# Queries and keys of the first attention group by seven block products, banks in turns, and the pooling projection from its last group to its first

## Chip, cores and metric

The kernel runs on one core of one Trainium2 chip. The metric is device time in microseconds of one execution: 1033.13 us, the median of three runs (1032.23 to 1033.27). TensorE (PE) multiplies, VectorE (DVE), ScalarE (ACT) and GpSimd (POOL) do the elementwise work, SyncE (SP) issues nearly all transfers.

## The reference, cut to what matters

One layer of a hybrid trunk on x of shape (1, 512, 1024), float32. A normed input u is projected by w_in into queries, keys and values of three attention groups (six heads of 64 each), a pooling input, the parts of a state space branch, and gates:

```
u = rmsnorm(x, ln1_g[i])
proj = u @ w_in[i]
q, k, v, pool_in, z, xbc, dt_raw, gate_pre = jnp.split(proj, split_idx, axis=-1)
...
scores = jnp.einsum("bhnqd,bhnkd->bhnqk", qb, kb).astype(jnp.float32) * scale + bias[:, None]
...
for gi, w in enumerate(POOL_WINDOWS):
    ...
    outs.append((c - shifted) / cnt - uf[..., sl])
d = jnp.stack(outs, axis=2).astype(u.dtype)
y = jnp.einsum("bsgc,gcd->bsgd", d, w_grp).reshape(b, s, POOL_WIDTH)
```

The attention scale is 0.125. The four pooling windows are 2, 4, 8 and 16 tokens, each on 256 of the 1024 pooling channels. After the three branches come a gated merge, an output projection, a gated convolutional FFN and a last norm.

## The kernel before, in words

Every float32 product is made of three TensorE products: each operand is split into a rounded high part and a low part (`wh`, `wl` of a weight, `uh`, `ul` of u), and `mm3` (L229) issues high by high, high by low, low by high, in this order, so that `wl` is read only in the last third of each chunk.

The work is a list of jobs (class `Job`, L73), written by `program()` (L1423) and run by the loop at L1634. A job has a weight tile `raw`, a `body` that issues its matmuls and evacuations, perhaps a `form` (the tile to use in place of a loaded one) and a `then` (what follows its split). Ahead of the body of job n, `prepare` (L1641) issues `low` of job n+1 (VectorE: raw minus high, L216, and then the job's `then`), `cast` of job n+2 (ScalarE: the high part, L196, in two halves that wait for the next two steps), and `fetch` of job n+3 (the load, L175; two `raw` buffers). TensorE, ScalarE, VectorE and GpSimd execute in the order in which the program issues; SyncE's order is left to the framework. `step()` (L157) is called between chunks of matmuls: it lets every generator in `running` and one of `waiting` go on by one `yield`. So elementwise work is spread over chunks.

The order of jobs: 4 of the pooling projection (`jobs_a`, L256, two chunks of 128 channels each, 24 matmuls of 512 columns a chunk), 2 of the values of group 0 (`v_jobs`, L588, 400 columns, four blocks of 12 matmuls each), 3 of queries and keys of group 0 (`qk_jobs`, L631), one that multiplies the pooled channels by pool_w (`pool_out_job`, L877), attention of group 0 between the chunks of the w_b projection, gates, the values of groups 1 and 2 (`v_pair`, L608), queries and keys of group 1 (`qk_sevens`, L650), and so on. The first two pooling jobs are issued by `begin` (L1543), interleaved with the turning of x.

`pool_evac(m)` (L852) takes pooling chunk m: ScalarE copies it out of the bank (L856), GpSimd doubles a window sum as often as its window needs (an addition L860 and a copy L861 for each doubling, then L863): once for m 0 and 1, twice for 2 and 3, three times for 4 and 5, four times for 6 and 7. Two steps later VectorE subtracts (`pd`, L869), ScalarE casts (L871), VectorE takes the low part (`pdl`, L872).

`v_pair` and `qk_sevens` halve u by tokens and by channels and use seven products of half-size blocks in place of eight. Their left sides are sums of blocks of u: `sums_of_u(p)` (L403) for p 0 to 3 makes them on VectorE (two additions L408, four half-width ones L326 to L329, two subtractions L335 and L336) with two ScalarE casts, in four steps, and before the change it runs once, beside the w_b jobs. The weights' sums are made in place by `diff` (L340, 128x1536). Two of the four weight quarters come into `W` (pool `ypool`, two buffers), two into `raw`. The products leave the bank by ScalarE copies and are added up on VectorE.

`attend(g)` (L720) adds the bias to the scores: for groups 0 and 2 the queries have been scaled by 0.125 on their way out of the bank (L642), for group 1 the scores are scaled as the bias is added (L758).

Of the kernel before, what the change touches and what calls it, by code (L numbers as in the profile page):

```python
# [13 lines left out]
OP = mybir.AluOpType  # L14
# [69 lines left out]
def trunk(ctx: ExitStack, tc, out, x, rel_bias, ln1_g, w_in, b_gate, w_a, pool_w, pool_scale, w_b,  # L84
# [258 lines left out]

    def sevens(quarter, c, side, W, emit):

        r1, r2, r3, r5 = {}, {}, {}, {}

        def job(j, load, form, use):  # L350
            def body(ws):
                wh, wl = ws
                parts = side(j)
                for i in range(2):
                    ps = MM("pb")
                    o = slice(i * P, (i + 1) * P)
                    mm3(ps[:, :c], lambda k: wh[:, k, :], lambda k: wl[:, k, :],
                        lambda k: parts[k][0][:, o], lambda k: parts[k][1][:, o], range(4), flip=True)
                    use(i, ps[:, :c])
                step()  # L360
            new = Job([load] if load is not None else [], 4, c, body)
            new.form = form
            if load is None:
                new.load = lambda: None
            return new

        def keep(r, name):
            def use(i, ps):
                r[i] = T(name)[:, :c]
                act.copy(r[i], ps)  # L370
            return use

        def p5(i, ps):
            keep(r5, "r5")(i, ps)
            dve.tensor_tensor(r2[i], r2[i], ps, OP.add)

        def p6(i, ps):
            dve.tensor_tensor(r1[i], r1[i], ps, OP.add)
            emit(0, 1, i, r1[i], r2[i])

        def p7(i, ps):
            r3[i] = T("r3")[:, :c]
            dve.tensor_tensor(r3[i], r1[i], ps, OP.add)
            emit(1, 1, i, r3[i], r5[i])

        one = job("A11", quarter(0, 0), None, keep(r1, "r1"))
        two = job("A12", quarter(1, 0), None, lambda i, ps: emit(0, 0, i, r1[i], ps))
        three = job(4, None, lambda: W[1], keep(r2, "r2"))
        one.then = lambda: diff(one.raw, W[0], one.raw)
        three.then = lambda: diff(W[0], W[1], W[0])  # L390
        two.then = lambda: diff(W[1], W[1], one.raw)
        yield one
        yield three
        yield two
        yield job(1, None, lambda: one.raw, p5)
        yield job(2, None, lambda: W[1], p6)
        yield job(3, None, lambda: W[0], p7)
        yield job("A22", None, lambda: diff(two.raw, two.raw, W[1]),
                  lambda i, ps: emit(1, 0, i, r3[i], ps))

# [18 lines left out]
    QUARTER = {"A11": (0, LO), "A12": (1, LO), "A22": (1, HI)}  # L419

# [187 lines left out]
    def v_pair():  # L608

        c, W = C_V + 384, []  # L610
        rows_ = lambda c0: w_in[:, c0:c0 + 384].rearrange("(k two p) c -> two p k c", two=2, p=P)
        quarter = lambda two, h: rows_(c + 384 * h)[two]

        def load():
            for two in range(2):
                W.append(ypool.tile([P, 4, S], F32, name="w3", tag="xs")[:, :, :384])
                sp.dma_start(W[two], quarter(two, 1))

        def emit(hi, right, i, a, ps):
            g, tb = 1 + right, 2 * hi + i  # L620
            t = T(f"v{g}")
            dve.tensor_tensor(t[:, :384], a, ps, OP.add)

            for n in range(4):
                if (g, n) not in V:
                    V[g, n] = T(f"vr{g}")
                sp.dma_start(V[g, n][32 * tb:32 * tb + 32, :384], t[n:P:4, :384])

        return load, sevens(quarter, 384, side_u, W, emit)
# [20 lines left out]
    def qk_sevens(g):  # L650


        W = []
# [3 lines left out]
        r1, r2, r3, r5 = {}, {}, {}, {}  # L657

        def load():
            for two in range(2):  # L660
                W.append(ypool.tile([P, 4, S], F32, name="w3", tag="xs")[:, :, :384])
                sp.dma_start(W[two], quarter(two, 1))

        def job(j, raw, form, use):
            def body(ws):
                wh, wl = ws
                parts = side_u(j)
                for i, ms in enumerate(chunks):
                    ps = MM("pq")
                    for n, m in enumerate(ms):  # L670
                        o = slice(m * P, (m + 1) * P)
                        mm3(ps[:, 256 * n:256 * n + 256], lambda k: wh[:, k, o], lambda k: wl[:, k, o],
                            lambda k: parts[k][0], lambda k: parts[k][1], range(4))
                    use(i, ps[:, :256 * len(ms)])
                step()
            new = Job([raw] if raw is not None else [], 4, 384, body)
            new.form = form
            if raw is None:
                new.load = lambda: None
            return new  # L680

        def keep(r):
            def use(i, ps):
                r[i] = T("rq")[:, :ps.shape[-1]]
                act.copy(r[i], ps)
            return use

        def emit(which, hi, i, a, b):

            for n, m in enumerate(chunks[i]):  # L690
                if (which, g, m) not in QK:
                    QK[which, g, m] = T(f"{which}{g}")
                view = (grouped if which == "q" else plain)(QK[which, g, m], g)
                piece = lambda t: perm(t[:, 256 * n:256 * n + 256], g)
                dve.tensor_tensor(view[:, :, 64 * hi:64 * hi + 64], piece(a), piece(b), OP.add)

        def p5(i, ps):
            keep(r5)(i, ps)
            dve.tensor_tensor(r2[i], r2[i], ps, OP.add)

        def p6(i, ps):
            dve.tensor_tensor(r1[i], r1[i], ps, OP.add)
            emit("k", 0, i, r1[i], r2[i])

        def p7(i, ps):
            r3[i] = T("rq")[:, :ps.shape[-1]]
            dve.tensor_tensor(r3[i], r1[i], ps, OP.add)
            emit("k", 1, i, r3[i], r5[i])

        one = job("A11", quarter(0, 0), None, keep(r1))  # L710
        two = job("A12", quarter(1, 0), None, lambda i, ps: emit("q", 0, i, r1[i], ps))
        three = job(4, None, lambda: W[1], keep(r2))
        one.then = lambda: diff(one.raw, W[0], one.raw)
        three.then = lambda: diff(W[0], W[1], W[0])
        two.then = lambda: diff(W[1], W[1], one.raw)
        return load, [one, three, two, job(1, None, lambda: one.raw, p5), job(2, None, lambda: W[1], p6),
                      job(3, None, lambda: W[0], p7), job("A22", None, lambda: diff(two.raw, two.raw, W[1]),
                                                          lambda i, ps: emit("q", 1, i, r3[i], ps))]

    def attend(g):  # L720
# [7 lines left out]
        def item(h, nb, bank):  # L728
# [21 lines left out]
            if g == 0 and total == 384:  # L750
                dve.tensor_tensor(sb[:, :256], ps[:, :256], b, OP.add)
                dve.tensor_tensor(sb[:, 256:384], ps[:, 256:384], b[:, P:], OP.add)
# [3 lines left out]
            else:  # L756
                n = len(bank)
                dve.scalar_tensor_tensor(sb.rearrange("p (n c) -> p n c", n=n),  # L758
                                         ps.rearrange("p (n c) -> p n c", n=n), 0.125 if g == 1 else 1.0,
# [663 lines left out]
    def program():  # L1423
        yield from jobs_a(w_in, C_POOL, 8, uhk, ulk, KD, pool_evac)
        yield Call(lambda: waiting.append(rows_of_bias()))
        yield from v_jobs(0)
        yield from qk_jobs(0)
        yield from pool_out_job()
        yield Call(lambda: attend(0))
        yield Call(lambda: waiting.insert(3, ssd_prep()))  # L1430
        for i, job in enumerate(branch_jobs(1, w_b, YB, 8, more=range(7))):
# [3 lines left out]
        load, pair = v_pair()  # L1435
        yield Call(load)
        yield from gate_jobs(1, 0, SPLIT)
        loads, qk = qk_sevens(1)
        for i, job in enumerate(pair):
            yield job  # L1440
            if i == 4:
                yield Call(loads)
# [100 lines left out]
    def begin(n, lo, hi, between=lambda early: None):  # L1543
# [157 lines left out]
```

## Time and profile before

| what | value |
|---|---|
| median of three runs | 1033.13 us (1032.23 to 1033.27) |
| the profiled execution | 1032.69 us, span in the profile 1030.9 us |
| busy in the span: TensorE, VectorE, ScalarE, GpSimd | 1019.8, 702.7, 490.2, 132.8 us |
| granted TensorE clock, mean | 0.999 |
| moved by DMA | 117.62 MB |
| largest VectorE group: low parts of weights, L216 | 95 instructions, 220.3 us |

The span is shorter than the execution by what lies before the first and after the last recorded instruction. In the views, a row of the chain or of the timeline begins with its start and its length in us, counted from the start of the span; merged rows end with the count of instructions. A square bracket tells idle time of the engine ahead of the row and who ended it. A row of windows gives for each engine its busy time in the stretch and its instructions. GpSimd's and VectorE's busy time includes time in which an instruction has been issued and waits inside the engine.

### The profile page before, as it was taken

The page shows a single profiled execution, that of the slowest core. Times are in us where ns is not written, and L with a number is a line of the kernel's source. Part 1 is how long each engine was busy: PE and PEld are TensorE (multiplying, and loading weights), DVE is VectorE, ACT ScalarE, POOL GpSimd, SP SyncE. Part 2 cuts the span into 40 slices and gives each one's busy share as a digit, 9 for nine tenths or more (in the row PEclk, how much of TensorE's full clock was granted, in tenths as well). Part 3 has the DMA queues.
Part 4 walks back from the last instruction along what each step waited for, and adds up shares of the span by engine and source line. Part 5 has one row for each costly group of instructions (what it writes and reads, how often), then busy time and mean ns, then how long its engine had stood idle before and what let it go on. Part 6 is the DMA issues. An engine that isn't in the chain of part 4 may idle for free.

```text
span 1030.9 us, 13254 instructions
## 1 busy us (share of the span) xinstructions
PE 1019.8 (99%) x5276; PEld 858.0 (83%) x5276; DVE 702.7 (68%) x932; ACT 490.2 (48%) x784; POOL 132.8 (13%) x114
## 2 busy tenths in 40 slices
PE   8999999999999999999999999999999999999997
PEld 8998877899888887788888888898888888888885
DVE  6553566788756648666688856767778668685756
ACT  6432545454674363567575324545444434433434
POOL 1770000000000001100044501101111100111002
PEclk9999999999999999999999999999999999999999
DMA  8444312034322354551253625543232233421322
GB/s 270 135 129 137 108 57 75 31 88 138 123 82 82 93 158 108 133 144 44 80 151 128 203 82 203 171 142 121 82 122 83 84 117 112 138 82 41 123 82 82
DMA packets 113357, 117.62 MB, mean 114 GB/s; under 512 B 5236, under 2 KB 97207, under 8 KB 113296
## 3 DMA queue, kind: packets, MB, share of 16 engines
q1 hardware_dynamic: 112703, 115.92, 36.4%
q8 instruction: 41, 0.67, 0.3%
q10 hardware_dynamic: 592, 0.86, 0.2%
q14 instruction: 21, 0.16, 0.1%
HBM read 112.97 MB, written 2.22 MB: 112 GB/s over the span
## 4 chain that ended last, share of the span: by engine, by line
PE 91%; DVE 4%; ACT 3%; issue 1%; DMA 1%; ACTq 0%; DVEq 0%
PE pa L237 30%; PE pu L237 22%; PE pb L237 12%; PE pd L237 7%; PE pqk L237 6%; PE pa L1552 2%; PE pq L237 2%; PE pu L1356 1%; PE ps L743 1%; PE pt L772 1%; PE ppw L237 1%; PE po L784 1%; DVE xs L1133 1%; DVE wl L216 1%; PE py L1057 1%
## 5 line engine op out<-in xcount | busy, mean ns | idle before, releaser
L216 DVE TENSOR_TENSOR wl<-raw,wh 128x2048 fp32r<-128x2048 f32 (+3 forms) x95 | 220.3, 2320 | 53.3 <-ACT wh L196 43.5
L196 ACT CAST wh<-raw 128x1024 fp32r<-128x1024 f32 (+3 forms) x188 | 187.6, 1017 | 48.3 <-DVE raw L341 18.0
L1251 DVE SCALAR_TENSOR_TENSOR hc<-pu,fcol,hc 128x510 f32<-128x510 f32 x88 | 65.8, 748 | 56.0 <-ACT hc L1248 54.4
L237 PE MATMUL pa<-uh,wh 128*128 128x512 f32 x384 | 98.4, 398 | 0.0
L237 PE MATMUL pa<-ul,wh 128*128 128x512 f32 x384 | 94.9, 389 | 0.0
L237 PE MATMUL pa<-uh,wl 128*128 128x512 f32 x384 | 94.8, 389 | 0.0
L237 PEld LDWEIGHTS pa<-ul,wh 128*128 128x128 f32 x384 | 72.1, 188 | 15.1
L237 PEld LDWEIGHTS pa<-uh,wl 128*128 128x128 f32 x384 | 72.1, 188 | 15.0
L237 PE MATMUL pu<-uh,wh 128*128 128x512 f32 (+1 forms) x352 | 83.6, 379 | 0.0
L237 PE MATMUL pu<-uh,wl 128*128 128x512 f32 (+1 forms) x352 | 83.5, 379 | 0.0
L237 PE MATMUL pu<-ul,wh 128*128 128x512 f32 (+1 forms) x352 | 83.5, 379 | 0.0
L237 PEld LDWEIGHTS pa<-uh,wh 128*128 128x128 f32 x384 | 70.3, 188 | 14.8 <-issue 1.0
L237 PEld LDWEIGHTS pu<-ul,wh 128*128 128x128 f32 x352 | 64.2, 188 | 12.5
L237 PEld LDWEIGHTS pu<-uh,wl 128*128 128x128 f32 x352 | 64.2, 188 | 12.5
L237 PEld LDWEIGHTS pu<-uh,wh 128*128 128x128 f32 x352 | 64.1, 188 | 12.4
L1248 ACT ACTIVATE hc<-pu,fcol,fcol 128x512 f32<-128x512 f32 x40 | 31.2, 780 | 80.5 <-PE pu L237 80.5
L1256 POOL TENSOR_TENSOR hc<-hc 128x512 f32<-128x512 f32 x22 | 30.8, 1402 | 289.1 <-DVE hc L1251 252.0
L1025 POOL TENSOR_TENSOR xd<-xc,dtz 128x512 f32<-128x512 f32 x6 | 6.4, 1063 | 355.9 <-issue 307.5
L765 ACT ACTIVATE sb<-sb,nmls 128x128 f32<-128x128 f32 (+1 forms) x72 | 30.1, 419 | 30.4 <-DVE nmls L762 17.7
L1149 ACT ACTIVATE sg<-pa,col 128x512 f32<-128x512 f32 x24 | 16.5, 688 | 45.5 <-PE pa L237 45.4
L1253 ACT ACTIVATE hc<-hc 128x512 f32<-128x512 f32 x22 | 13.9, 632 | 39.9 <-DVE hc L1251 39.9
L907 DVE SCALAR_TENSOR_TENSOR xs<-pa,col,xs 128x509 f32<-128x509 f32 (+2 forms) x24 | 18.0, 749 | 18.7 <-ACT xs L903 18.2
(373 smaller groups left out, 1868.0 us busy)
## 6 DMA issues: line engine op xcount, KB each, us to landing
raw<-in_w_in_dram SPq DMA_DIRECT2D x25, 1024.0 KB, 5.5
raw<-in_ffn_w_up_dram SPq DMA_DIRECT2D x22, 1024.0 KB, 5.2
raw<-in_w_o_dram SPq DMA_DIRECT2D x8, 1024.0 KB, 6.6
raw<-in_ffn_w_down_dram SPq DMA_DIRECT2D x8, 1024.0 KB
raw<-in_w_in_dram SPq DMA_DIRECT2D x14, 512.0 KB, 3.9
raw<-in_w_in_dram SPq DMA_DIRECT2D x6, 768.0 KB
raw<-in_w_b_dram SPq DMA_DIRECT2D x4, 1024.0 KB, 5.2
al<-ad SPq DMA_DIRECT2D x16, 256.0 KB, 7.7
```

What stands on the lines that cost most here:

```text
L196: act.copy(job.high[:, :, o], job.raw[:, :, o])
L216: (eng or dve).tensor_tensor(l[:, :, o], job.raw[:, :, o], h[:, :, o].bitcast(F32), OP.subtract)
L237: pe.matmul(ps, l, r, start=first and n == 0, stop=last and n == total - 1, skip_group_check=onto)
L743: pe.matmul(pss[i][:, o:o + w * P], q[r, n * P:(n + 1) * P], k[r, kb * P:(kb + w) * P], start=True, stop=True)
L765: act.activation(sb[:, off:off + w * P], sb[:, off:off + w * P], AF.Exp, bias=nm[:, n, h:h + 1], accum_out=ls[:, n, h:h + 1])
L907: dve.scalar_tensor_tensor(t[:, sh:], ps[:, :S - sh], col[:, o_cw + 12 * k + m:o_cw + 12 * k + m + 1], t[:, sh:], OP.mult, OP.add)
L1149: act.activation(s, ps, AF.Sigmoid, bias=col[:, o:o + 1])
L1248: act.activation(t, ps, AF.Identity, bias=ff["c1"][:, ff["b"] + m:ff["b"] + m + 1], scale=fw(2, m))
L1251: dve.scalar_tensor_tensor(t[:, sh:], ps[:, :S - sh], fw(k, m), t[:, sh:], OP.mult, OP.add)
L1253: act.activation(t, t, AF.Silu)
L1256: pool.tensor_tensor(a, a, t, OP.mult)
L1552: pe.matmul(first[2 * n + j][:, lo:hi], a[:, k, j * P:(j + 1) * P], b[:, k, lo:hi], start=a is wh and b is uh and k == 0, stop=a is wl and ...
```

## The change

- Queries and keys of group 0 are no longer made by three jobs of 512-column chunks but by `qk_sevens(0)`: seven products of 36 matmuls of 256 columns. For this `sums_of_u` is run a second time, early: it is started ahead of the third pooling job. The two quarters in `W` are loaded at that place, and their difference is taken (`first`) ahead of the second job of the values of group 0.
- `v_pair` and `qk_sevens` are both written over `in_banks`. Two pairs of banks, A and B, are used in turns by the seven products, in the order one, three, six, five, seventh, two, four; the products six, seventh and four add onto what bank pair A holds. A result goes straight to its place by a ScalarE copy and later pieces are added there by VectorE, in place of separate copies of each product.
- The queries of group 0 leave unscaled; `attend(0)` scales the scores as it adds the bias.
- The four pooling jobs run in reverse, so that chunks come as 6, 7, 4, 5, 2, 3, 0, 1.

The core of the diff (the two functions that it replaces are printed above):

```diff
+    def in_banks(quarter, c, outs, both, chunks=None):
...
+        W, A, B = [], [], []
...
+        def job(j, raw, form, banks, use, onto=False, between=None):
+            def body(ws):
+                wh, wl = ws
+                parts = side_u(j)
+                if not A:
+                    for b in (B, A):
+                        b.extend(MM("pq") for _ in range(2))
+                for i in range(2):
+                    for n, m in enumerate(chunks[i] if chunks else (i,)):
+                        o = slice(m * P, (m + 1) * P)
+                        if chunks:
+                            mm3(banks[i][:, 256 * n:256 * n + 256], lambda k: wh[:, k, o],
+                                lambda k: wl[:, k, o], lambda k: parts[k][0], lambda k: parts[k][1],
+                                range(4), onto=onto or n > 0)
+                        else:
+                            mm3(banks[i][:, :c], lambda k: wh[:, k, :], lambda k: wl[:, k, :],
+                                lambda k: parts[k][0][:, o], lambda k: parts[k][1][:, o],
+                                range(4), onto=onto, flip=True)
+                    outs(*use, i, banks[i][:, :256 * (n + 1) if chunks else c])
+                    if j == 1:
+                        both(i)
+                    if i == 0 and between:
+                        between()
+                    step()
...
+        one = job("A11", quarter(0, 0), None, A, (0, 0, False),
+                  between=lambda: diff(W[1], W[1], one.raw))
+        three = job(4, None, lambda: W[1], B, (1, 0, False))
+        six = job(2, None, lambda: one.raw, A, (1, 0, True), onto=True)
+        five = job(1, None, lambda: W[1], B, (1, 1, False))
+        seventh = job(3, None, lambda: W[0], A, (1, 1, True), onto=True)
+        two = job("A12", quarter(1, 0), None, B, (0, 0, True))
+        four = job("A22", None, lambda: two.raw, A, (0, 1, False), onto=True)
+        one.then = lambda: dve.tensor_tensor(one.raw, W[0], one.raw, OP.add)
+        two.then = lambda: diff(two.raw, two.raw, one.raw)
+        return load, lambda: diff(W[0], W[1], W[0]), [one, three, six, five, seventh, two, four]
...
+        def outs(right, hi, more, i, ps):
             for n, m in enumerate(chunks[i]):
...
+                to = view("qk"[right], m, hi)
+                piece = ps[:, 256 * n:256 * n + 256]
...
+                if more:
+                    dve.tensor_tensor(to, to, piece, OP.add)
+                else:
+                    act.copy(to, piece)
...
-                dve.tensor_tensor(sb[:, :256], ps[:, :256], b, OP.add)
-                dve.tensor_tensor(sb[:, 256:384], ps[:, 256:384], b[:, P:], OP.add)
+                dve.scalar_tensor_tensor(sb[:, :256], ps[:, :256], 0.125, b, OP.mult, OP.add)
+                dve.scalar_tensor_tensor(sb[:, 256:384], ps[:, 256:384], 0.125, b[:, P:], OP.mult, OP.add)
...
     def program():
-        yield from jobs_a(w_in, C_POOL, 8, uhk, ulk, KD, pool_evac)
+        load, first, qk = qk_sevens(0)
+        for i, job in enumerate(reversed(list(jobs_a(w_in, C_POOL, 8, uhk, ulk, KD, pool_evac)))):
+            if i == 2:
+                yield Call(load)
+                yield Call(lambda: running.extend(after(p, sums_of_u(p)) for p in range(4)))
+            yield job
         yield Call(lambda: waiting.append(rows_of_bias()))
-        yield from v_jobs(0)
-        yield from qk_jobs(0)
+        for i, job in enumerate(v_jobs(0)):
+            if i == 1:
+                yield Call(first)
+            yield job
+        yield from qk
         yield from pool_out_job()
...
-                pool_evac(2 * n + j, first[2 * n + j])
+                pool_evac(6 - 2 * n + j, first[2 * n + j])
```

`v_pair` gets its load, its `first` and its products from the same function; its `first` now runs ahead of the second gate job, and that of `qk_sevens(1)` ahead of the last product of `v_pair`.

More of the change, by code (lines that the diff above doesn't have):

```diff
@@ L342, in diff @@
         return out
[L344 to L399, printed above, removed]
     US = {}
@@ L419, in trunk, with load @@
     QUARTER = {"A11": (0, LO), "A12": (1, LO), "A22": (1, HI)}
+    def in_banks(quarter, c, outs, both, chunks=None):
+        W, A, B = [], [], []
+        def load():
+            for two in range(2):
+                W.append(ypool.tile([P, 4, S], F32, name="w3", tag="xs")[:, :, :c])
+                sp.dma_start(W[two], quarter(two, 1))
+        def job(j, raw, form, banks, use, onto=False, between=None):
[22 more added lines that the diff above has]
+                    step()
+            new = Job([raw] if raw is not None else [], 4, c, body)
+            new.form = form
+            if raw is None:
+                new.load = lambda: None
+            return new
+        one = job("A11", quarter(0, 0), None, A, (0, 0, False),
[9 more added lines that the diff above has]
+        return load, lambda: diff(W[0], W[1], W[0]), [one, three, six, five, seventh, two, four]
@@ L608, in v_pair, with both, rows_out @@
     def v_pair():
-        c, W = C_V + 384, []
+        c = C_V + 384
         rows_ = lambda c0: w_in[:, c0:c0 + 384].rearrange("(k two p) c -> two p k c", two=2, p=P)
[L612 to L619, printed above, removed]
-            g, tb = 1 + right, 2 * hi + i
-            t = T(f"v{g}")
-            dve.tensor_tensor(t[:, :384], a, ps, OP.add)
+        kept = {}
+        def outs(right, hi, more, i, ps):
+            g, tb = 1 + right, 2 * hi + i
+            if more:
+                dve.tensor_tensor(kept[g, tb], kept[g, tb], ps, OP.add)
+            else:
+                kept[g, tb] = T(f"v{g}")[:, :384]
+                act.copy(kept[g, tb], ps)
+            if not right and hi or more and (not right or hi):
+                rows_out(g, tb)
+        def both(i):
+            dve.tensor_tensor(kept[2, i], kept[2, i], kept[2, 2 + i], OP.add)
+            rows_out(2, i)
+        def rows_out(g, tb):
+            t = kept[g, tb]
             for n in range(4):
@@ L656, in qk_sevens @@
         chunks = ((0, 1), (2,))
[L657 to L680, printed above, removed]
@@ L697, in p5 @@
[L697 to L711, printed above, removed]
@@ L712, in qk_sevens, with view @@
[L712 to L718, printed above, removed]
+        def view(which, m, hi):
+            if (which, g, m) not in QK:
+                QK[which, g, m] = T(f"{which}{g}")
+            t = (grouped if which == "q" else plain)(QK[which, g, m], g)
+            if g == 0:
+                return t[:, 256 * hi:256 * hi + 256] if which == "k" else t[:, 2 * hi:2 * hi + 2]
+            return t[:, :, 64 * hi:64 * hi + 64]
@@ L720, in attend, with both @@
+        def both(i):
+            for m in chunks[i]:
+                lo, hi = view("k", m, 0), view("k", m, 1)
+                dve.tensor_tensor(lo, lo, hi, OP.add)
+        return in_banks(quarter, 384, outs, both, chunks)
     def attend(g):
@@ L1434, in program @@
             yield job
[L1435 to L1438, printed above, removed]
+        yield Call(loadv)
+        for i, job in enumerate(gate_jobs(1, 0, SPLIT)):
+            if i == 1:
+                yield Call(firstv)
+            yield job
+        load, first, qk = qk_sevens(1)
         for i, job in enumerate(pair):
+            if i == 4:
+                yield Call(load)
+            if i == 6:
+                yield Call(first)
             yield job
-            if i == 4:
-                yield Call(loads)
         yield from qk
```

26 lines of the change are left out of this document (11 added, 15 removed).

## The prediction, made before the changed kernel was run

> **What bounds the kernel now.** I read the page first: busy time and the shares of the chain that ended last.
>
> ```profile
> span 1030.9 us, 13254 instructions
> ...
> PE 1019.8 (99%) x5276; PEld 858.0 (83%) x5276; DVE 702.7 (68%) x932; ACT 490.2 (48%) x784; POOL 132.8 (13%) x114
> ...
> PE 91%; DVE 4%; ACT 3%; issue 1%; DMA 1%; ACTq 0%; DVEq 0%
> ```
>
> TensorE has work for 1019.8 of 1030.9 us. A matmul that is saved comes off the end, and any wait that is added to TensorE goes straight onto it. Next the chain in order of time, at the stages that the change touches (start, length):
>
> ```profile
> 36.84 21.79 PE pa L237 x96
> 58.63 4.39 PE pb L237 x24
> ...
> 78.01 32.64 PE pqk L237 x144
> 110.65 10.88 PE ppw L237 x48
> ...
> 206.33 29.14 PE pb L237 x168
> 235.47 17.34 PE pq L237 x144
> ```
>
> Pooling, values, queries and keys of group 0 and the pool_w job follow each other without a gap. The value stage runs from 58.63 to 78.01. Then I asked for the windows from GpSimd's first pooling instruction to the end of that stage (start:end, length, then TensorE, its loads, VectorE, ScalarE, GpSimd, clock, DMA):
>
> ```profile
> 31.66:36.00 4.34, 4.34 (x39) 4.34 (x38) 2.04 (x1) 2.21 (x2) 4.26 (x5) 1.00 0.01 2
> 36.00:58.00 22.00, 22.00 (x101) 18.33 (x101) 14.40 (x13) 9.83 (x14) 20.60 (x26) 1.00 0.45 123
> 58.00:72.20 14.20, 14.20 (x77) 12.84 (x76) 7.66 (x7) 4.39 (x6) 13.56 (x19) 1.00 0.29 77
> 72.20:78.00 5.80, 5.80 (x33) 5.80 (x32) 3.59 (x3) 3.04 (x8) 0.03 (x1) 1.00 0.91 234
> ```
>
> TensorE is the bound, but GpSimd has almost no free time until 72.2 (38.4 of 40.5 us), though it is 13% busy over the span. VectorE looks free: 14.40 + 7.66 + 3.59 = 25.7 of the 42 us after 36. The timeline of both shows that it isn't:
>
> ```profile
> 32.64 0.19 POOL L861 COPY psw<-pu 128x1 f32<-128x1 f32 x1
> ...
> 33.96 2.29 DVE L216 TENSOR_TENSOR wl<-raw,wh 128x2048 fp32r<-128x2048 f32 x1 [7.69 <-ACT wh L196]
> 34.04 2.26 POOL L861 COPY psw<-pu 128x1 f32<-128x1 f32 x1
> ...
> 46.85 1.04 POOL L860 TENSOR_TENSOR psw<-pu 128x511 f32<-128x511 f32 x1
> 46.94 1.50 DVE L869 SCALAR_TENSOR_TENSOR pd<-psw,pu 128x512 f32<-128x512 f32 x1 [0.37 <-POOL psw L863]
> ```
>
> The same one-column copy of GpSimd takes 0.19 us alone and 2.26 when a VectorE subtraction runs, and both end together. `pd` takes 1.50 when it is issued behind an addition of GpSimd, against 0.69 alone (below). Here the two engines work in turns, instruction by instruction.
>
> **The change part by part.** *TensorE.* 144 matmuls of 512 columns took 32.64 us, 0.2267 each. Those of 256 columns took 17.34/144 = 0.1204 each, so the new stage needs 7 x 36 x 0.1204 = 30.34. That saves 2.3 us, not the eighth (4.1), because a half-width matmul costs more than half. The values of groups 1 and 2 keep their 168 matmuls.
>
> *Queries and keys of group 1.*
>
> ```profile
> 260.86 1.75 DVE L216 TENSOR_TENSOR wl<-raw,wh 128x1536 fp32r<-128x1536 f32 x1
> ```
> ```profile
> 262.66 0.74 PE L237 MATMUL pq<-uh,wl 128*128 128x256 f32 x4 [0.27 <-DVE wl L216]
> ```
> ```profile
> 262.66 3.62 PE pq L237 x28
> ```
>
> The stage ends at 266.28; 252 matmuls from 235.47 would end at 265.81. The wait behind `wl` costs 0.5. The new order has 12 additions on VectorE in place of 18, and keeps four weight sums, one of which leaves the stage; I count the 0.5 as gained (bounds 0 and 0.5: there is no other gap).
>
> *New VectorE work ahead of the first new product.* Prices, from the sums that run today beside the gates, with GpSimd silent:
>
> ```profile
> 189.99 0.68 DVE L335 TENSOR_TENSOR sal<-sa,sah 128x512 fp32r<-128x512 f32 x1
> ...
> 191.19 0.42 DVE L326 TENSOR_TENSOR sa<-uf 128x256 f32<-128x256 f32 x1
> ...
> 192.66 1.29 DVE L408 TENSOR_TENSOR uf<-uh,ul 128x512 f32<-128x512 f32 x2
> 193.86 0.67 DVE L800 COPY nmT<-pst 6x512 f32<-6x512 f32 x1
> ...
> 201.27 1.76 DVE L341 TENSOR_TENSOR raw<-w,raw 128x1536 f32<-128x1536 f32 x1
> 202.94 0.68 DVE L1151 TENSOR_TENSOR yo<-yo,sg 128x512 f32<-128x512 f32 x1
> ```
>
> From start to start: two subtractions 1.20, four combinations 1.47, two additions 1.20, a weight sum 1.67. Four sets are 15.5. Counting steps from the third pooling job on (two in each pooling and each value job), set p adds in step p+1, combines in p+2, is cast in p+3, subtracts in p+4. So all but the last subtractions (1.2) stand on VectorE ahead of `low` of the first product, which is issued behind step 6. `first` adds 1.67 and that `low` shrinks by 0.6 (1536 columns, not 2048). Together 14.3 + 1.7 - 0.6 = 15.4 us.
>
> *How much of it hides.* The end of the pooling work before the change:
>
> ```profile
> 61.30 1.81 DVE L216 TENSOR_TENSOR wl<-raw,wh 128x1600 fp32r<-128x1600 f32 x1
> ...
> 69.08 1.14 DVE L548 COPY rv<-psr 6x512 f32<-6x512 f32 x2
> ...
> 72.26 0.69 DVE L869 SCALAR_TENSOR_TENSOR pd<-psw,pu 128x512 f32<-128x512 f32 x1 [2.04 <-POOL psw L863]
> 73.64 0.69 DVE L872 TENSOR_TENSOR pdl<-pd,pdh 128x512 fp32r<-128x512 f32 x1 [0.69 <-ACT pdh L871]
> 74.25 2.29 DVE L216 TENSOR_TENSOR wl<-raw,wh 128x2048 fp32r<-128x2048 f32 x1
> ```
> ```profile
> 69.28 1.03 POOL L860 TENSOR_TENSOR psw<-psw 128x508 f32<-128x508 f32 x1
> ...
> 70.53 1.27 POOL L860 TENSOR_TENSOR psw<-psw 128x504 f32<-128x504 f32 x1
> ...
> 72.01 0.22 POOL L863 TENSOR_TENSOR psw<-psw,ramp 128x16 f32<-128x16 f32 x1
> ```
>
> An undisturbed doubling on GpSimd is 1.25 (69.28 to 70.53), so its 20 doublings and 8 closings are 26.6. VectorE has in the same time two `low` of 2.29, two of 1.81, seven `pd` and seven `pdl` of 0.69 and 1.14: 19.0. Together 45.6, and 31.66 to 72.23 are 40.6: a factor of 0.89 for what overlaps. The eight `pd` each wait for GpSimd, in order, ahead of the `low` that follows them, so added VectorE work moves the whole row of both engines: 15.4 x 0.89 = 13.7. The slack is small: `low` of the first qk weights ends at 76.54 today. The first product's third group of four matmuls, the first to read `wl`, would come at 78.01 + 8 x 0.1204 = 78.97. 13.7 - 2.4 = 11.3 us of waiting, spread over `low` of both value jobs and of the first product. Bounds: 0, if the sums fit into the 16 us in which VectorE does nothing; 14.4, if nothing overlaps and the last two chunks, with GpSimd done, each add the 0.69 wait for ScalarE. I take 11.3, by the factor of the same stretch. Behind each late `low` the bank evacuations of the stage are queued, and TensorE waits for the `low` itself.
>
> *The reverse order.* Chunks 6 and 7 now come first, and in ScalarE's order the cast of the fourth pooling job's weights stands behind `pdh` of the second chunk:
>
> ```profile
> 40.17 1.91 ACT L196 CAST wh<-raw 128x2048 fp32r<-128x2048 f32 x1
> ```
>
> Today that chunk's window is 2 and the cast starts at 40.17. Chunks 6 and 7 are 8 doublings, 10.0 us, plus the `low` of 2.29 and 1.4 us of chunk 6's `pd` and `pdl` in between: GpSimd ends near 45.5, `pd` and `pdh` near 47.6, the cast near 49.5. The job's first matmul is due at 36.84 + 10.9 = 47.7. So TensorE waits 1.8 us there (bounds 0 and 3). This is not added: the later `low` waits pass it by.
>
> *Costed at nothing.* The stage of seven products: VectorE has 7 `low`, 3 weight sums, 12 additions of 256 (0.55 each: the row below, three in 1.66), about 23 of 30 us, and GpSimd is silent then; without that cover each late `low` would cost its excess. Scaled scores: the same two instructions with another operation. Transfers: the early load of two quarters stands today in the same place for `v_pair`, and `v_pair`'s own has some 70 us. The pool_w tile can load only when the sixth product's `then` is done: I count a margin of 1.4 us (cost 0 to 2).
>
> ```profile
> 248.06 1.66 DVE L695 TENSOR_TENSOR q<-rq,pq 128x256 f32<-128x256 f32 x3
> ```
>
> *Sum.* 1030.9 - 2.3 - 0.5 + 11.3 = 1039.4 of span. The profiled execution took 1032.69, 1.8 more than its span, and the median is 0.4 above that: 1039.4 + 1.8 + 0.4 = **1041.6 us**.
>
> **A rule on the clock.** No stretch of this trace has a wait of several us amid matmuls; only its opening is slow:
>
> ```profile
> 1.05 4.57 PE L1510 MATMUL pa<-ones 128*128 128x128 f32 x24 [1.05 <-DVE ones L1501]
> ...
> 9.43 2.05 PE L1569 MATMUL uT<-diag,xin 128*128 128x128 f32 x16 [0.32 <-DVE diag L1581]
> ```
>
> 24 matmuls took 0.190 each there, against 0.128 for the like shape later. The Trainium skill, "TensorE: Matmul & The Clock Gate", section "HAM oscillation", says that a gap of over some 3.4 us returns TensorE to half clock. By it each long wait would add an estimated 1.7 us. As a rival I price it by the rows: 4.6 us at 0.190 for 0.128 lose 1.5 a wait.
>
> **Rivals.**
> 1. *The sums fit.* VectorE has 16 us without work from 36 to 78, and the sums need 15.4. If its additions can slip between those of GpSimd, nothing waits but what the reverse order was to clear: 1033.1 - 2.3 - 0.5 = 1030.3, faster. It decides if less than 2.4 us of the added work pushes the row. For it: 16 is over 15.4. Against it: the 2.26 and 1.50 above.
> 2. *Only the reverse order bites*: the sums fit, but the cast behind `pdh` comes 1.8 late: 1032.1, no change.
> 3. *The late `low`, and slow matmuls after the three waits*: two to three times 1.5 on top: near 1045. For it: the opening. Against it: the clock reads 1.00 even there.
> 4. *The saving isn't there*, if adding onto a bank that is being read holds the products: each bank has a whole product (4.3 us) before it is used again, so this is small, and I leave it inside the range.
>
> **How the numbers follow.** A measurement of this kernel can tell about 0.2% (2.1 us) from no change. Forecast 0.66; rival 1 0.10; rival 2 0.07; rival 3 0.17. Faster: rival 1, 0.10. Within: rival 2 and a little of the forecast's low end, 0.09. Slower: 0.81. The range leaves out rivals 1 and 2 and goes from 1034 (a wait of 4 us, most of it overlapped) to 1047 (14.4 us and the clock).
>
> **What would show it.** Right: TensorE idle ahead of `pb` and of the first `pq` matmuls, released by `wl` of L216; a first product that starts 8 to 14 us later than 78.0; GpSimd and VectorE full from 46 to 90, with copies of GpSimd well over 0.19 us beside L408 and L326 to L329; a short wait near 47.7 that ends with L196; a qk stage of some 30.3 us. Wrong: no gap there; or L408 at its 0.65 with GpSimd's additions at 1.04 in the same time, which would mean that these additions don't take turns.

## The result and the profile after

The changed kernel takes 1047.52 us, the median of four runs (1047.17 to 1048.07), beside 1033.09 us for the kernel before. The ratio is 1.0139, interval 1.0127 to 1.0151: 14.4 us slower. Forecast were 1041.6 us and a range up to 1047. The sign and the place were right; the loss was 5.9 us larger.

The profiled execution took 1047.33 us. Its page, in the same lines as before, with the granted clock in 40 slices (tenths of full speed) ahead of the chain's shares:

```profile
span 1045.5 us, 13547 instructions
...
PE 1023.4 (98%) x5384; PEld 865.6 (83%) x5384; DVE 726.7 (70%) x969; ACT 502.9 (48%) x817; POOL 133.2 (13%) x114
...
PEclk9988999999999999999999999999999999999999
...
PE 87%; DVE 5%; DMA 3%; POOL 2%; ACT 2%; issue 1%; SPq 0%; ACTq 0%; DVEq 0%; POOLq 0%
```

TensorE should be 2.3 us less busy and is 3.6 us busier. So the loss isn't idle time alone: some matmuls ran slower, and the clock's row says where, in the third and fourth slice (52 to 105 us). The timeline of TensorE, the rows that were preceded by a wait and some of those behind them, from the pooling stage to the pool_w job:

```profile
49.49 2.11 PE L237 MATMUL pa<-uh,wh 128*128 128x512 f32 x8 [1.68 <-ACT wh L196]
51.44 1.99 PE L237 MATMUL pa<-ul,wh 128*128 128x512 f32 x8
...
68.23 1.70 PE L237 MATMUL pb<-wl,uh 128*128 128x400 f32 x4 [6.09 <-DVE wl L216]
69.72 1.54 PE L237 MATMUL pb<-wh,uh 128*128 128x400 f32 x4
...
79.68 0.89 PE L237 MATMUL pb<-wh,ul 128*128 128x400 f32 x4
81.31 1.00 PE L237 MATMUL pb<-wl,uh 128*128 128x400 f32 x4 [0.73 <-DVE wl L216]
...
89.97 0.74 PE L237 MATMUL pq<-uh,wh 128*128 128x256 f32 x4 [1.07 <-ACT dtr L599]
...
93.58 1.22 PE L237 MATMUL pq<-uh,wl 128*128 128x256 f32 x4 [2.39 <-DVE wl L216]
...
98.02 1.05 PE L237 MATMUL pq<-ul,wh 128*128 128x256 f32 x4
98.87 0.69 PE L237 MATMUL pq<-uh,wl 128*128 128x256 f32 x4
99.40 0.64 PE L237 MATMUL pq<-sbh,wh 128*128 128x256 f32 x4
...
127.20 0.73 PE L237 MATMUL ppw<-pdh,wl 128*128 128x512 f32 x2 [0.80 <-DVE wl L216]
```

Each of the three stages ahead of the second product waits for a late high or low part. Read from start to start, four matmuls take 0.85 us at 98.02, and 0.48 from 99.40 on, where the second product begins. So the 28 that follow the last long wait took 5.82 us (93.58 to 99.40); at 0.1204 they would have taken 3.37. The same windows as before, moved on to 110 (TensorE, its loads, VectorE, ScalarE, GpSimd, clock, DMA):

```profile
36.00:58.00 22.00, 20.32 (x93) 16.61 (x92) 12.50 (x11) 7.23 (x10) 21.03 (x29) 1.00 0.27 75
58.00:72.20 14.20, 8.11 (x33) 7.32 (x32) 12.76 (x17) 3.83 (x7) 10.16 (x13) 0.76 0.17 56
72.20:78.00 5.80, 5.80 (x32) 4.54 (x31) 5.77 (x10) 2.18 (x4) 2.18 (x3) 1.00 0.00 0
78.00:95.00 17.00, 12.80 (x69) 11.93 (x68) 14.82 (x20) 8.69 (x19) 0.00 (x0) 0.92 0.45 126
95.00:110.00 15.00, 15.00 (x113) 15.00 (x112) 10.97 (x11) 6.43 (x12) 0.00 (x0) 0.87 0.20 57
```

The clock drops to 0.76, 0.92 and 0.87 where the waits end. VectorE shows the other half: in the first window it works 12.50 us, less than the 14.40 of before, and from 72.2 to 78 it is full while GpSimd has little left (2.18 us). Its timeline shows both:

```profile
39.14 1.51 DVE L838 SCALAR_TENSOR_TENSOR pd<-psw,pu 128x512 f32<-128x512 f32 x1 [2.83 <-POOL psw L832]
...
45.47 1.51 DVE L838 SCALAR_TENSOR_TENSOR pd<-psw,pu 128x512 f32<-128x512 f32 x1 [3.10 <-POOL psw L832]
...
55.51 2.12 DVE L351 TENSOR_TENSOR uf<-uh,ul 128x512 f32<-128x512 f32 x2
...
61.58 1.30 DVE L327 TENSOR_TENSOR sa<-sa,uf 128x256 f32<-128x256 f32 x1
...
65.52 2.65 DVE L216 TENSOR_TENSOR wl<-raw,wh 128x1600 fp32r<-128x1600 f32 x1
...
91.78 1.75 DVE L216 TENSOR_TENSOR wl<-raw,wh 128x1536 fp32r<-128x1536 f32 x1
```
```profile
49.79 2.25 POOL L830 COPY psw<-psw 128x4 f32<-128x4 f32 x1
...
68.30 0.26 POOL L832 TENSOR_TENSOR psw<-psw,ramp 128x2 f32<-128x2 f32 x1
72.66 1.06 POOL L829 TENSOR_TENSOR psw<-pu 128x511 f32<-128x511 f32 x1 [4.09 <-ACT pu L825]
```

The first sum (L351, L408 before) comes at 55.51: it is queued behind `pd` of the third chunk, and the first two `pd` have waited 2.83 and 3.10 us for the long windows. Two additions beside GpSimd take 2.12 us in place of 1.28, a combination 1.30 in place of 0.42. GpSimd has done seven of its eight windows by 68.56, and `low` of the first product ends at 93.53: for 25 us VectorE works almost alone.

### The profile page after: what moved, and what is told of

Read it like the earlier page. It is cut to its first block, busy times and chain, and to the rows that moved or that the text cites. A ratio compares the mean times of both kernels' runs of the same rounds, so it can differ in the third digit from the quotient of the medians.

```text
span 1045.5 us, 13547 instructions
## 1 busy us (share of the span) xinstructions
PE 1023.4 (98%) x5384; PEld 865.6 (83%) x5384; DVE 726.7 (70%) x969; ACT 502.9 (48%) x817; POOL 133.2 (13%) x114
## 4 chain that ended last, share of the span: by engine, by line
PE 87%; DVE 5%; DMA 3%; POOL 2%; ACT 2%; issue 1%; SPq 0%; ACTq 0%; DVEq 0%; POOLq 0%
PE pa L237 31%; PE pu L237 22%; PE pq L237 7%; PE pd L237 7%; PE pb L237 7%; PE pqk L237 3%; PE pa L1534 2%; POOL psw L829 2%; DVE wl L216 1%; PE ps L712 1%; PE pt L741 1%; PE po L753 1%; PE ppw L237 1%; DMA al<-ad 1%; ACT wh L196 1%; POOL psw L830 1%
## 5 line engine op out<-in xcount | busy, mean ns | idle before, releaser
L237 PEld LDWEIGHTS pu<-uh,wh 128*128 128x128 f32 x352 | 64.1, 188 | 12.7 <-ACT uh L453 0.3
L216 DVE TENSOR_TENSOR wl<-w,wh 128x1536 fp32r<-128x1536 f32 (+1 forms) x15 | 30.6, 2038 | 6.6 <-ACT wh L196 6.6
```

Of the source, the lines that this page charges most:

```text
L216: (eng or dve).tensor_tensor(l[:, :, o], job.raw[:, :, o], h[:, :, o].bitcast(F32), OP.subtract)
L237: pe.matmul(ps, l, r, start=first and n == 0, stop=last and n == total - 1, skip_group_check=onto)
```

## The experiments

In the diffs, - is the changed kernel, + the experiment; for e2 the - side is the kernel before.

**The order of the pooling jobs.**

```diff
-for i, job in enumerate(reversed(list(jobs_a(w_in, C_POOL, ...)))):
+for i, job in enumerate(jobs_a(w_in, C_POOL, ...)):
...
-pool_evac(6 - 2 * n + j, first[2 * n + j])
+pool_evac(2 * n + j, first[2 * n + j])
```

> The changed kernel with the pooling jobs in their old order. Theory (VectorE's early sums share a row with GpSimd's window sums, and the row is too long): the work of the row is the same, so the low part of the first product's weights still ends near 93 us and the first product still waits; only the short wait for the cast of the fourth pooling job (1.7 us) goes. 1045 to 1049 us. Rival (the reverse order is what delays VectorE): nearly all of the loss goes, 1031 to 1035 us.

Measured: 1042.87 us, ratio 1.0096 (1.0081 to 1.0111). That is between the two, and below what was expected: the sums without the reverse order cost some 10 us, and the reverse order 4.65 on top (between the medians; the four runs here go from 1041.77 to 1044.00). Its waits on TensorE:

```profile
77.08 1.70 PE L237 MATMUL pb<-wl,uh 128*128 128x400 f32 x4 [6.24 <-DVE wl L216]
...
89.32 0.73 PE L237 MATMUL pq<-uh,wl 128*128 128x256 f32 x4 [1.29 <-DVE wl L216]
```

The third group of the first product comes at 89.32, 4.26 us ahead of the changed kernel's 93.58. To see why, take for each kernel the window from 36.00 to the end of `low` of the first product of group 0 (76.54, 93.53, 89.27). Before, after, and this experiment:

```profile
36.00:76.60 40.60, 40.60 (x201) 35.57 (x201) 25.64 (x23) 17.26 (x28) 34.19 (x44) 1.00 0.44 117
```
```profile
36.00:93.60 57.60, 45.62 (x217) 39.01 (x215) 44.44 (x55) 21.92 (x39) 33.38 (x44) 0.93 0.26 77
```
```profile
36.00:89.30 53.30, 45.78 (x217) 40.16 (x215) 46.23 (x54) 21.95 (x39) 39.06 (x44) 0.94 0.28 83
```

VectorE's busy time grows by 18.8 and 20.6 us (third figure after the length, 44.44 and 46.23 against 25.64); its time without work was 14.96 and becomes 13.16 and 7.07. So the changed kernel fills 1.8 us of its gaps and pushes the rest: 18.8 - 1.8 = 17.0 us later. In the old order 7.9 us of the gaps are filled: 20.6 - 7.9 = 12.7 later. The reverse order does not make VectorE's work dearer (it is 1.8 less). It has 6.1 us more without work, and the two waits for long windows shown above, 2.83 and 3.10, are 5.9 of them: they come ahead of the first sum, and no sum can go into them. A version that begins the sums earlier was not run.

**The reverse order alone**, in the kernel before:

```diff
-yield from jobs_a(w_in, C_POOL, 8, uhk, ulk, KD, pool_evac)
+yield from reversed(list(jobs_a(w_in, C_POOL, 8, uhk, ulk, KD, pool_evac)))
...
-pool_evac(2 * n + j, first[2 * n + j])
+pool_evac(6 - 2 * n + j, first[2 * n + j])
```

> The kernel before with only the pooling jobs reversed. Theory: TensorE waits some 1.7 us for the cast of the fourth pooling job's weights, near 47.7 us, and for nothing else: 1034.5 to 1036 us. Rival (the reverse order is the main cause): 1040 us or more. A second rival (the wait is passed by later on): 1033.1 us.

Measured: 1035.16 us, ratio 1.0018 (1.0009 to 1.0028). TensorE has one new long wait:

```profile
49.81 2.12 PE L237 MATMUL pa<-uh,wh 128*128 128x512 f32 x8 [1.70 <-ACT wh L196]
```

So without the sums the reverse order costs about the forecast's 1.8 us (0.9 to 2.9 by the interval); with them 4.65.

**The sums left out.** The products of group 0 read plain halves of u; the sums of blocks are not made, so the queries and keys of group 0 are not the reference's.

```diff
-yield Call(lambda: running.extend(after(p, sums_of_u(p)) for p in range(4)))
+yield Call(plain_sides)
...
+def plain_sides():
+    for p in range(4):
+        for j, (two, half) in {1: (0, LO), 2: (0, HI), 3: (1, LO), 4: (1, HI)}.items():
+            US[j, p] = uh[:, 2 * p + two, half], ul[:, 2 * p + two, half]
```

> The changed kernel without the sums of u for group 0: four of the seven products take plain halves of u in their place (group 0's queries and keys are then other numbers), so that 15.4 us of VectorE work and eight casts leave the pooling and value stages, and all else stays. Theory: the three long waits go and the clock stays up. What stays is 2.3 and 0.5 us saved, 0.9 us saved at the merge of the groups, against 1.9 us for the reverse order and 1.1 us for the late pool_w tile: 1032.4 us, from 1031 to 1034. Rival (banks in turns, adding onto banks, or the rest of the seven products cost the time): 1042 us or more.

Measured: 1033.41 us, ratio 1.0005 (0.9996 to 1.0015): 14.1 us less than the changed kernel. The whole loss hangs on the sums.

**GpSimd's window sums left out**, the pooling result with them; the sums of u stay.

```diff
-nxt = T("psw")
-pool.tensor_tensor(nxt[:, sh:], cur[:, sh:], cur[:, :S - sh], OP.add)
-pool.tensor_copy(nxt[:, :sh], cur[:, :sh])
-cur, sh = nxt, sh * 2
+sh = sh * 2
```

> The changed kernel without GpSimd's window sums (the pooling branch then uses unsummed channels; only the short closing multiplication stays on GpSimd). VectorE has all its work, the early sums too. Theory (the two engines work in turns): VectorE alone is done with the low part of the first product's weights near 77.5 us, before it is due at 79, so no long wait: 1030.5 us, from 1030 to 1033. Rival (VectorE has too much to do by itself, GpSimd doesn't matter): low still ends near 90 us, 1042 us or more.

Measured: 1032.53 us, ratio 0.9996 (0.9986 to 1.0005). What is left of the waits, one pair of additions on VectorE, and the window to the end of `low` of the first product (79.80):

```profile
79.85 0.74 PE L237 MATMUL pq<-uh,wl 128*128 128x256 f32 x4 [0.37 <-DVE wl L216]
...
111.53 0.73 PE L237 MATMUL ppw<-pdh,wl 128*128 128x512 f32 x2 [0.86 <-DVE wl L216]
```
```profile
52.29 1.28 DVE L351 TENSOR_TENSOR uf<-uh,ul 128x512 f32<-128x512 f32 x2
```
```profile
36.00:79.80 43.80, 43.48 (x220) 38.24 (x218) 35.48 (x54) 21.90 (x39) 2.81 (x6) 1.00 0.35 99
```

The loss also vanishes when the sums stay and GpSimd is silent. So it is neither engine's work by itself but their standing in one line. In the changed kernel the like window is 57.60 us long, 13.8 more (the row to 93.60 above), and VectorE's figures tell the two parts of them. It is busy 9.0 us longer (44.44 against 35.48) with the same instructions: the two engines hold each other up (two additions take 1.28 here, 2.12 above). And it is without work 4.8 us longer (13.16 against 8.32): `pd` waits for a window, and the sums wait behind `pd`.

**Banks in turns for group 1 only.** Group 0's queries and keys as before the change, pooling in the old order:

```diff
-yield from qk
+yield from qk_jobs(0)
...
-yield Call(lambda: running.extend(after(p, sums_of_u(p)) for p in range(4)))
```

> The changed kernel with group 0's queries and keys made as before (no early sums) and the pooling jobs in their old order: what is left of the change is banks in turns for the values of groups 1 and 2 and the queries and keys of group 1. Theory: no long wait, the 0.5 us wait in the qk stage of group 1 goes or shrinks, and the 0.9 us at the merge of the groups may go: 1031.7 to 1032.8 us, a little under before. Rival (banks in turns cost something): over 1033.5 us.

Measured: 1032.85 us beside 1033.04 for the kernel before, ratio 0.9997 (0.9988 to 1.0006). A gain of half a microsecond is below what the runs can tell.

**TensorE kept busy.** Matmuls of 512 columns that nobody reads are added where the waits were: 26 ahead of the first matmuls of the values that read `wl`, and 5 and 11 about the first product.

```diff
+def busy(n):
+    ps = SM("busy")
+    for _ in range(n):
+        pe.matmul(ps, uh[:, 0, :P], uh[:, 0, :], start=True, stop=True)
...
 for a, b in ((wh, xh), (wh, xl), (wl, xh)):
+    if a is wl and spare:
+        busy(spare.pop())
```

> The changed kernel with matmuls of no use put into TensorE's two longest waits: 26 of 512 columns ahead of the first reading of the low part in the first value job, 5 ahead of and 11 within the first product. Theory (the matmuls after these waits are slow because TensorE was idle): the 28 matmuls after the wait in the first product go at 0.12 us in place of 0.21, the granted clock stays at 1.00, and 2.4 us come back: 1045.1 us, from 1044.3 to 1046. Rival (they are slow for another reason, or the clock doesn't matter to the end): 1047.5 us.

Measured: 1047.77 us, ratio 1.0137 (1.0124 to 1.0151): as the changed kernel. TensorE, from the second value job on:

```profile
81.31 1.47 PE L246 MATMUL pb<-wl,uh 128*128 128x400 f32 x4 [2.23 <-DVE wl L216]
82.58 1.53 PE L246 MATMUL pb<-wh,uh 128*128 128x400 f32 x4
...
92.37 2.68 PE L234 MATMUL busy<-uh 128*128 128x512 f32 x11
94.89 0.64 PE L246 MATMUL pq<-uh,wl 128*128 128x256 f32 x4
...
98.24 0.64 PE L246 MATMUL pq<-sbh,wh 128*128 128x256 f32 x4
```

With no idle time ahead of them, the 28 matmuls of the first product take 3.35 us (94.89 to 98.24) in place of 5.82, at a granted clock of 1.00; in the changed kernel it was 0.54 from 93.58 to 99.40. So the slow pace does come from the waits. But the expected gain of time did not come. The added matmuls ran 1.3 us past the moment at which `wl` was ready, so the second product begins only 1.16 earlier than in the changed kernel, and at the end of the span nothing of it is left (1045.4 against 1045.5). The trace shows where it goes:

```profile
131.01 0.73 PE L246 MATMUL ppw<-pdh,wh 128*128 128x512 f32 x2 [0.23 <-DVE ybl L865]
...
582.31 0.50 PE L246 MATMUL pa<-al,wh 128*128 128x512 f32 x1 [0.56 <-DVE al L824]
```

The matmuls behind the pool_w job start 0.7 us earlier than in the changed kernel, at 136.60 in place of 137.31: a bank of that job whose evacuation (`ybl`) comes late has taken most of the rest. That lead is still there at 500 us and ends with a wait for `al`, which the profiled execution of the changed kernel doesn't have.

**More room for the sums.** The pooling in its old order, the sums begun at the last value job, and the seven products put behind the pool_w job and the first w_b job; the first four chunks of `gate_jobs(1)` get a step in their middle:

```diff
+yield from jobs_a(w_in, C_POOL, 8, uhk, ulk, KD, pool_evac)
+yield Call(load)
...
+wb = list(branch_jobs(1, w_b, YB, 8, more=range(7)))
+yield Call(first)
+yield wb[0]
+yield from qk
```

> The seven products for group 0 kept, but behind the pool_w job and the first w_b job, pooling in its old order, the early sums started with the last value job, when GpSimd is nearly done; attention of group 0 moves behind with them, and the first two gate jobs get a step in the middle of each chunk, to give it room. Theory: the sums then meet an idle GpSimd and some 22 us of products with little VectorE work, so the three long waits go: 1030 to 1034 us, if VectorE keeps up with attention later. Rival (the sums are too much for VectorE wherever they stand): 1038 us or more.

Measured: 1038.41 us, ratio 1.0045 (1.0033 to 1.0058), between the two again. The three waits are gone, others came:

```profile
107.65 0.75 PE L237 MATMUL pq<-sbh,wl 128*128 128x256 f32 x4 [1.22 <-DVE wl L216]
...
193.70 1.63 PE L753 MATMUL po<-sb,v 128*64 128x128 f32 x14 [3.20 <-ACT sb L742]
```

Attention of group 0 runs in the steps of the w_b jobs and has lost some of them, which would explain the 3.20 us that `po` waits for it; no run tests this. The loss of some 5 us was not added up stage by stage.

**Room from the gates.** Instead of a w_b job, two chunks of `gate_jobs(0)` go ahead of the products, behind the pool_w job. The pooling keeps its old order, and the sums begin ahead of the last value job:

```diff
+yield from pool_out_job()
+yield from gate_jobs(0, 0, 2)
+yield from qk
...
-yield from gate_jobs(0)
+yield from gate_jobs(0, 2, more=(0, 1))
```

> Pooling in its old order; the pool_w job and the first two chunks of the gate jobs of g go ahead of the seven products, and the sums of group 0 start ahead of the last value job. Theory (the loss comes from VectorE's sums standing in one order with GpSimd's window sums, and from nothing in the products themselves): GpSimd is done with the pooling by 73, the sums cost their lone price (L408's additions near 0.65 each, the combinations 0.42) beside some 22 us of other products, attention keeps the w_b jobs that it has today, and no wait over 2 us is left: 1030 to 1032.5 us, 0.6 to 3 below the kernel before. Rival (the place of group 0's products is tight whatever is put ahead of them, because the two chunks that leave the later gate stage take cover from the SSD work, as the w_b job did from attention): 1034 us or more, with a wait of TensorE of 2 us or more after 180.

Measured: 1033.86 us, ratio 1.0008 (0.9998 to 1.0017): no long wait, but no gain either, where 1030 to 1032.5 was expected. Two waits of TensorE are left:

```profile
85.28 0.73 PE L237 MATMUL ppw<-pdh,wh 128*128 128x512 f32 x2 [1.67 <-DVE ybl L856]
108.51 0.38 PE L237 MATMUL pq<-sbl,wh 128*128 128x256 f32 x1 [1.46 <-DVE sbl L336]
```

The first is a bank of the pool_w job whose evacuation (`ybl`) is queued behind sums and a `low`, the second the last subtraction of the sums. Together they are 3.1 us, a little over the 2.8 that the products save.

**Four gate chunks, and the sums later.** e11 puts four chunks ahead. e12 also begins the sums behind the value jobs and takes the first weights' sum behind the pool_w job. What e12 adds to e10:

```diff
 for i, job in enumerate(v_jobs(0)):
-    if i == 1:
-        yield Call(first)
-        yield Call(lambda: running.extend(after(p, sums_of_u(p)) for p in range(4)))
     yield job
+yield Call(lambda: running.extend(after(p, sums_of_u(p)) for p in range(4)))
 yield from pool_out_job()
+yield Call(first)
-yield from gate_jobs(0, 0, 2)
+yield from gate_jobs(0, 0, 4, more=(0, 1))
...
-yield from gate_jobs(0, 2, more=(0, 1))
+yield from gate_jobs(0, 4, more=(0, 1, 2, 3))
```

> As the kernel behind two gate chunks, with four gate chunks ahead of the products, the first two of them with a step in their middle; the four that stay behind get such a step too. Theory (the 1.46 us wait ahead of the second product was VectorE's own backlog, which 11 us more of products with little VectorE work clears; the 1.67 in the pool_w job is a bank evacuation queued behind two additions of 1.29 and stays): 1031.5 to 1033 us, one wait of some 1.7 us left. Rival (four chunks fewer leave the SSD stage short of cover): 1035 or more with waits of TensorE after 640.

> The same with the sums begun behind the value jobs instead of within them, and the weight sum of the first product behind the pool_w job. Theory: the evacuation in the pool_w job isn't held any more, so that no wait over 1 us is left: 1030 to 1032 us, 1 to 3 below the kernel before, which is what TensorE's shorter stages give. Rival (the backlog only moves on to the first product, as the sums start 5 us later): 1032.5 or more, with a wait by wl or by a subtraction at the first or second product. Second rival: 1035 or more with waits after 640.

Measured: e11 1033.10 us, ratio 0.9997 (0.9988 to 1.0006); e12 1031.40 us, ratio 0.9983 (0.9974 to 0.9993). In e11 the wait at `sbl` is gone and that of the pool_w job is still there. The profiled execution of e11 was its longest (1035.74 us) and has another wait, 1.26 us at 688.81, which e12's has not. The timeline of TensorE in e11, its one wait between 40 and 420 us:

```profile
86.89 0.73 PE L237 MATMUL ppw<-pdh,wh 128*128 128x512 f32 x2 [1.64 <-DVE ybl L856]
```

In e12 neither is there. The first line of its page, and its chain at the stages that moved:

```profile
span 1029.1 us, 13572 instructions
```
```profile
65.72 13.39 PE pb L237 x72
79.11 10.88 PE ppw L237 x48
90.00 21.76 PE pa L237 x96
111.75 30.23 PE pq L237 x252
```

Values, pool_w, four gate chunks and the seven products follow each other without a gap. This is the only version that is faster than the kernel before: 1.8 us by the ratio (0.7 to 2.7), with the same products and the same sums as the changed kernel, and the pooling in its old order. The gain is less than the 2.1 us that the forecast took for the least that can be told, but the interval leaves out no change, and the spans agree (1029.1 against 1030.9).

## Why the prediction was right and wrong, step by step

*TensorE's saving* (30.34 in place of 32.64): right. From 99.40 the six further products take 25.91 us (to 125.31) for 216 matmuls, 0.1200 each; e12's 252 take 30.23.

*Queries and keys of group 1* (0.5 gained): right. The chain of the changed kernel runs through the values of groups 1 and 2 and this stage in one piece, 168 + 252 matmuls:

```profile
222.23 59.41 PE pq L237 x420
```

The same work took 59.95 us before (206.33 to 266.28). As a gain of the whole time it was too small to be measured (e5).

*Added VectorE work and its overlap* (15.4 x 0.89 = 13.7, waiting 11.3): right in size for the old pooling order. e1 moves `low` of the first product by 12.7 us, from 76.54 to 89.27, and its third group from 78.97 to 89.32, 10.35 of waiting. That the sizes meet is partly luck: the 15.4 us of instructions lengthen VectorE's busy time by 20.6, since the engines hold each other up, and 7.9 of that falls into gaps. The factor 0.89 knows neither number.

*The reverse order* ("This is not added: the later `low` waits pass it by"): **this is the step that failed.** The forecast priced the order as one late cast on ScalarE, 1.8 us, and let the larger wait swallow it. That holds for the cast (1.68 at 49.49, 1.70 in e2). But the order also decides how much of the sums can overlap, and the factor 0.89 was taken from a stretch in the old order, with short windows first. With the long ones first, VectorE waits 2.83 and 3.10 us for its first two `pd`, with the sums queued behind them. Apart from these 5.9 us it has 7.2 us without work until `low` of the first product, as in the old order (7.07). So 5.9 us of gaps are lost to the sums, and 1.8 come back: GpSimd is done earlier, and VectorE's busy time is that much less than in e1. The chain ends 17.0 us late in place of 13.7; the waiting is 14.6 us (78.97 to 93.58) in place of 11.3. That is close to the upper bound, 14.4, but not for its reason: the bound was for 15.4 us of work with no overlap and two waits of 0.69, and here it is 18.8 us of busy time, of which 1.8 fall into gaps.

*Slow matmuls after the waits* (rival 3, 1.5 a wait): partly right. It was a term to add to the forecast and was left out of its sum. Behind the 6.09 wait the matmuls were slow too, but there the next `wl` was late anyway: in e7, where they ran at full pace, the wait at 81.31 grew from 0.73 to 2.23. After the last wait the 28 matmuls took 2.45 us more, at a moment when TensorE's next stages follow without a gap. That taking this away shortens the whole was not shown: e7 got 1.16 of it back and lost it again. The rows of the trace before could not show this; the clock read 1.00 even in the opening on which the rival was priced.

*The pool_w job* (cost 0 to 2, taken as nothing): 0.80 us.

*Sum* for the changed kernel's span: -2.3 for the products, -0.5 for group 1, +14.6 for the waits, +2.45 for slow matmuls, +0.8 for pool_w, and -0.6 for a wait of the kernel before that is not there in this execution. Together +14.4, where the span grew by 14.6 (1030.9 to 1045.5). So the forecast's miss of 5.9 us is 3.3 of longer waits, 2.45 of slow matmuls and 0.8 at pool_w, less the 0.6. The wait that is not there, in the timeline of the kernel before:

```profile
567.67 0.50 PE L237 MATMUL pa<-al,wh 128*128 128x512 f32 x1 [0.58 <-DVE al L846]
```

*Rivals 1, 2 and 4* are out: the sums did not fit (e1, e3), the cast alone explains 2 us (e2), and the products do save what they should (e12).

## What to carry to other kernels

When work is added to an engine whose queue is in order, ask not how much time it has without work but which of its gaps the new work can reach: a gap ahead of an instruction that waits for another engine is lost to all that stands behind it. A change of order that costs 2 us by itself can cost 5 beside such work, so the overlap has to be worked out again in the new order and not taken from the old one. If a saving on the bounding engine is 3 us and needs 15 us of work elsewhere, place that work first: here the same products and sums went from 14 us slower to 2 us faster by being put behind other products, with the pooling in its old order.

## What the runs showed of the hardware

Waits of 2.2 us and more slowed TensorE's next matmuls for some 4 to 5.5 us. After 6.09 us of idle time groups of four `pb` took 1.70 and 1.54 us, against 0.89 at 79.68. In e7 a single wait of 2.23 us was enough (1.47 and 1.53 for four at 81.31 and 82.58), while the 1.68 us at 49.49 in the changed kernel left the pace nearly as it was (2.11 for eight against 1.99), as did 1.29 in e1 (0.73 for four against 0.64). The Trainium skill, "TensorE: Matmul & The Clock Gate", section "HAM oscillation", names a gap of over some 3.4 us. The 6.09 agrees; the 2.23 does not, and the measurement decides: in these traces the longest wait without a slow pace is 1.70 us (e2), the shortest with one 2.23. Whether the edge is the same elsewhere isn't shown.

VectorE's two-input additions and GpSimd's work held each other up, down to a copy of four columns that took 2.25 us (49.79) in place of 0.19. The Trainium skill, "SBUF — State Buffer", section "Who interferes with whom", states that a VectorE instruction with two inputs there contends with a GpSimd instruction that reads it; the pairs above agree (2.12 for 1.28, 1.30 for 0.42).
